# The end of a two-layer streaming encoder: second half of the tokens turned by TensorE before the last scaling

## The chip, the cores and the metric

One core of a Trainium2 chip runs the whole kernel. Its engines are TensorE (PE, matmuls), VectorE (DVE), ScalarE (ACT), GpSimd (POOL) and SyncE (SP, which here only issues DMAs). Each takes its instructions in the order in which they were written. The metric is the device time of one launch in microseconds (us), the median of several runs.

## The reference

The input is x, 512 tokens by 1024 features, in float32. Two layers follow, each a token mixer and a gated feed-forward network (FFN), both behind an RMS norm and both added to x. The last norm gives the output:

```python
def rmsnorm(x, g):
    xf = x.astype(jnp.float32)
    y = xf * lax.rsqrt(jnp.mean(xf * xf, axis=-1, keepdims=True) + EPS)
    return (y * g.astype(jnp.float32)).astype(x.dtype)

def conv_ffn(h, w_up, conv_w, conv_b, w_down):
    u, v = jnp.split(h @ w_up, 2, axis=-1)
    u = causal_dwconv(u, conv_w, conv_b)
    return (jax.nn.gelu(u, approximate=False) * v) @ w_down

for l in range(2):
    x = x + mixer(rmsnorm(x, mix_norm[l]))
    x = x + conv_ffn(rmsnorm(x, ffn_norm[l]), ...)
return rmsnorm(x, final_norm)
```

So every token needs the sum of the squares of its 1024 features, its inverse root, and then each feature is multiplied by that root and by the feature's gain in final_norm.

## The kernel before

The kernel keeps x with the features on the partitions: eight tiles x[0] to x[7] of 128 features by 512 tokens, all in one buffer xall (x3 is its view as 8 tiles). Every product is done in three matmul passes on high and low parts of the operands (accumulate, L252, and seven_product). Weights are loaded, split into the two parts and used block by block.

The work of the FFN is an order written out by hand: each step is entered with a time by at(t, step), and run_plan sorts the steps by these times and issues them. The order of the instructions of TensorE, VectorE and ScalarE is thereby fixed. Loads and stores that SP issues are queued in the order in which they are written.

At the end of the second FFN the down-projection makes the eight feature tiles one after the other. Each is multiplied by the norm factors rs and added to x[j] (add_x, L810 and L811). Then finish(j) is called, which for this layer is last(j, half). For the tiles 0 to 6 that squares x[j] and adds the squares to acc (square_acc, L288 and L289). For the tiles 0 to 5, x[j] is also multiplied by its gain, in place, on ScalarE (L1480).

The last tile, x[7], is made in two halves of 256 tokens (down_half): 42 matmuls for the first half, then add_x and last(7, 0) for it, then 42 matmuls for the second half, add_x and last(7, 1). In last(7, half):

- ScalarE squares the half tile (L1483). PE sums the columns of acc and of these squares over the partitions by a matmul with ones (L1490), giving two columns of 128 sums, tokens on partitions.
- rsqrt_small takes the inverse root: VectorE makes v (L293), ScalarE a first y (L295), and three small VectorE instructions refine it (L299 to L301).
- spread_small (L327) multiplies by an identity on PE so that the root of each token stands on all partitions (bc).
- scale_out multiplies pairs of feature tiles by it on VectorE (L1514; for the tiles 6 and 7, whose gain is still missing, L1517) and stores each pair, 256 KB, in rows of 256 tokens (L1520).

Work can be put between the matmuls: after(n, fn) runs fn at the n-th tick from now, and down_half ticks once for each group of seven matmuls. For the first half the sums and the root are put behind 2 groups and the spread behind 4, so they stand between the matmuls of the second half. The scaling of the first half is issued in last(7, 1): two pairs ahead of the second half's root, one between its steps and one behind it.

Of the kernel before, what the change touches and what calls it, by code (L numbers as in the profile page):

```python
# [7 lines left out]
F32 = mybir.dt.float32  # L8
# [3 lines left out]
AF = mybir.ActivationFunctionType  # L12
ALU = mybir.AluOpType

P = 128
T = 512
D = 1024
KD = D // P
# [7 lines left out]
EPS = 1e-6  # L26
# [29 lines left out]
NPLAIN = NF - KD  # L56
# [15 lines left out]


@with_exitstack
def trunk_kernel(ctx, tc, xT, cols, gain0, w_lead, w_ab, w_pool, w_abo, w_vg, w_qk, w_r, w_g2, w_go, w_up, w_dn, w_ds, outT):
    nc = tc.nc
    V, S, G, PE = nc.vector, nc.scalar, nc.gpsimd, nc.tensor

# [5 lines left out]
    sp = ctx.enter_context(tc.tile_pool(name="sp", bufs=2))  # L84
    ps = ctx.enter_context(tc.tile_pool(name="ps", bufs=8, space=bass.MemoryType.PSUM))

    def slot(dt=F32, name="s"):
        return big.tile([P, T], dt, tag="s", name=name)
# [17 lines left out]
    def bank(name="ps"):  # L106
        return ps.tile([P, T], F32, tag="ps", name=name)
# [3 lines left out]
    x = [xall[:, k * T : (k + 1) * T] for k in range(KD)]  # L111
# [4 lines left out]
    def col(name, i=0):  # L116
        c = COLS[name] + i
        return colt[:, c : c + 1]
# [30 lines left out]
    ones = cp.tile([P, P], F32, tag="ones", name="ones")  # L149
# [5 lines left out]
    warm = ps.tile([P, T], F32, tag="ps", name="warm")  # L155
# [6 lines left out]
    eps_t = cp.tile([P, 1], F32, tag="eps", name="eps_t")  # L162
# [3 lines left out]
    ident = cp.tile([P, P], F32, tag="ident", name="ident")  # L166
# [77 lines left out]
    def after(n, fn):  # L244
        pending.append((done[0] + n, fn))
# [6 lines left out]
        for p in due:  # L252
            p[1]()

    def accumulate(out, wh, wl, ah, al, first=True, last=True, step=None, cut=0, loose=False):
        n = len(ah)
        if cut:
            accumulate(out, wh, wl, ah[:cut], al[:cut], first, False)
            accumulate(out, wh[:, cut:, :], wl[:, cut:, :], ah[cut:], al[cut:], False, last)
            return  # L260
        for i, (w, a) in enumerate(((wh, ah), (wh, al), (wl, ah))):
            for k in range(n):
                PE.matmul(  # L263
                    out, w[:, k, :], a[k], start=first and i == 0 and k == 0, stop=last and i == 2 and k == n - 1,
                    skip_group_check=loose,
                )
            if step:
                step()

# [13 lines left out]
    def square_acc(k, acc, ts=slice(0, T)):  # L283
        if k == 0 and ts.start == 0:
            S.activation(acc[:, ts], x[0][:, ts], AF.Square)
            return
        sq = slot(name="sq")
        S.activation(sq[:, ts], x[k][:, ts], AF.Square)  # L288
        V.tensor_tensor(acc[:, ts], acc[:, ts], sq[:, ts], ALU.add)  # L289

    def rsqrt_small(dst, ssum, n, width, between=None):
        v = sp.tile([P, n], F32, tag=f"v{n}", name="v")
        V.tensor_scalar(v, ssum, 1.0 / width, EPS, ALU.mult, ALU.add)  # L293
        y = sp.tile([P, n], F32, tag=f"y{n}", name="y")
        S.activation(y, ssum, AF.Abs_reciprocal_sqrt, bias=eps_t, scale=1.0 / width)  # L295
        if between:
            between()
        t = sp.tile([P, n], F32, tag=f"t{n}", name="t")
        V.tensor_tensor(t, y, v, ALU.mult)  # L299
        V.scalar_tensor_tensor(t, t, -0.5, y, ALU.mult, ALU.mult)  # L300
        V.scalar_tensor_tensor(dst, t, 1.5, y, ALU.add, ALU.mult)  # L301
# [22 lines left out]
    def spread_small(y, n):  # L324
        b = bank("bc")[:, : n * P]
        for c in range(n):
            PE.matmul(  # L327
                b[:, c * P : (c + 1) * P], y[:, c : c + 1].broadcast_to([P, P]), ident, start=True, stop=True
            )
        return b  # L330
# [28 lines left out]
    def conv3(u, wname, bname, j, nj):  # L359
        tap = conv_steps(u, wname, bname, j, nj)  # L360
        return [tap(i) for i in range(3)][0]

    def scaled(o, rs, tag):
        u = slot(name=tag)
        V.tensor_tensor(u, o, rs, ALU.mult)
        return u
# [244 lines left out]
    def ffn(l, acc, mixed, finish, ahead, halves_last=False):  # L611
# [141 lines left out]
        o, late, ops = {}, {}, {}  # L753
# [8 lines left out]
        def down_half(half, k0, kt):  # L762
            if half == 0:
                late[k0] = ready.pop(0)
            h, lo = late[k0]
            ts = slice(half * H, half * H + H)
            if k0 == 0:
                o["half"] = bank("dn")
            accumulate(
                o["half"][:, :H], h, lo,  # L770
                [m[:, ts] for m in mh[k0 : k0 + kt]], [m[:, ts] for m in ml[k0 : k0 + kt]],
                k0 == 0, k0 + kt == NPLAIN, step=tick,
            )

        def down_seven(p, base):
# [53 lines left out]
        t = base + 9 * UNIT  # L829
# [3 lines left out]
        def plain_down(j):  # L833
            nonlocal t
            while blocks and (blocks[0][0] == j or (j == 0 and blocks[0][0] < 4)):
                jj, k0, kt = blocks.pop(0)
                first = t < base + 9.5 * UNIT
                block(t - 16.0, t - (9.3 if first else 6.0), t - (7.0 if first else 4.5))
                if halves_last and jj == KD - 1:
                    at(t, lambda a=(0, k0, kt): down_half(*a))  # L840
                    t += 1.5 * kt * MM
                else:
                    at(t, lambda a=(jj, k0, kt): down(*a))
                    t += 3 * kt * MM
# [26 lines left out]
        if halves_last:  # L871
            at(t, lambda: add_x(KD - 1, o["half"][:, :H], lo_t))
            at(t, lambda: finish(KD - 1, 0))
            for k0, kt in zip(DOWN_AT, DOWN_K):
                at(t, lambda a=(1, k0, kt): down_half(*a))
                t += 1.5 * kt * MM
            at(t, lambda: add_x(KD - 1, o["half"][:, :H], hi_t))
            at(t, lambda: finish(KD - 1, 1))
        else:
            done_right(HK - 1, t + 0.3)  # L880
# [5 lines left out]
    acc = slot(name="acc")  # L886
# [30 lines left out]
    with tc.manual_schedule(engines=set(planned)):  # L917
# [6 lines left out]
        for n in range(2, 5):  # L924
            k = lead[n][1]
# [62 lines left out]
    for j in range(4):  # L988
        pc = project(xh, xl, "pc") if j else first_pc
        px = project(xh, xl, "px")  # L990
        c = scaled(pc, rs, "u")
        d = scaled(px, rs, "v")
        V.tensor_tensor(c, c, d, ALU.mult)
        a = conv3(c, "sc_w", "sc_b", j, 4)
        pb = project(xh, xl, "pb")
        b = scaled(pb, rs, "v")
        V.tensor_tensor(b, b, a, ALU.mult)
        split(y_h[4 + j], y_l[4 + j], b)
    acc = slot(name="acc")
# [13 lines left out]
    acc = total[0]  # L1013
# [273 lines left out]
    t = 0.0  # L1287
# [15 lines left out]
    first = True  # L1303
    for b, (n, ks) in enumerate(zip(VG_COLS, VG_K)):
        k0 = 0
# [158 lines left out]
    acc = slot(name="acc")  # L1464
# [3 lines left out]
    mixed = mix_out("go", "ffn1", acc, 2, 2)  # L1468

    squares = []  # L1470

    def last(j, half=None):
        if not squares:
            squares.append(slot(name="acc"))
        acc = squares[0]
        ts = slice(0, T) if half is None else slice(half * 256, half * 256 + 256)
        if half is None:
            square_acc(j, acc)
            if j < KD - 2:
                S.activation(x[j], x[j], AF.Copy, scale=col("fin", j))  # L1480
            return
        sq = slot(name="sq")[:, :256]
        S.activation(sq, x[j][:, ts], AF.Square)  # L1483
        y2 = sp.tile([P, 2], F32, tag="y2", name="y2")

        def one(between=None):
            b = bank("ss")
            for i, t in enumerate((acc[:, ts], sq)):
                for c in range(2):
                    PE.matmul(  # L1490
                        b[:, c : c + 1], t[:, c * P : (c + 1) * P], ones[:, 0:1],
                        start=i == 0 and c == 0, stop=i == 1, skip_group_check=True,
                    )
            rsqrt_small(y2, b[:, :2], 2, D, between)

        def two():
            return ts, spread_small(y2, 2)

        if half:
            scale_out(*spread[0], (0, 2))  # L1500
            one(lambda: scale_out(*spread[0], (4,)))
            scale_out(*spread[0], (6,))
            scale_out(*two(), range(0, KD, 2))
        else:
            after(2, one)
            after(4, lambda: spread.append(two()))

    spread = []

    def scale_out(ts, b, ks):  # L1510
        for k in ks:
            o3 = x3[:, k : k + 2, ts]
            if k < KD - 2:
                V.tensor_tensor(o3, o3, b[:, None, :].broadcast_to([P, 2, 256]), ALU.mult)  # L1514
            else:
                for i in range(2):
                    V.scalar_tensor_tensor(  # L1517
                        x[k + i][:, ts], x[k + i][:, ts], col("fin", k + i), b, ALU.mult, ALU.mult
                    )
            (nc.scalar if k % 4 and ts.start else nc.sync).dma_start(  # L1520
                outT[k * P : (k + 2) * P, ts].rearrange("(a p) t -> p a t", p=P), o3
            )

    ffn(1, acc, mixed, last, 0, True)


_OUTS = [((D, T), "float32")]


def _blocks(w, n):  # L1530
# [72 lines left out]
```

## Time and profile before

| | |
|---|---|
| median of 3 runs | 1003.15 us (1002.39 to 1003.23) |
| profiled execution | 1002.91 us |
| its span | 1001.0 us |
| mean granted TensorE clock | 0.996 of full speed |
| busy, share of the span | PE 99%, DVE 85%, ACT 61%, POOL 9% |

A profile records one execution. Its span runs from the first to the last recorded instruction; 1.9 us of the execution's time lie outside it. In timelines a row gives the start and the duration in us, the engine, the line and operation, the tiles (out<-in) with their shapes and the number of instructions that were merged; in brackets stands how long the engine was idle before and what released it. SPq and ACTq are the queues from which SP and ScalarE issue DMAs. A matmul's recorded duration contains its way through the array, so rows of consecutive matmuls overlap.

### The profile page before, as it was taken

How to read it: one execution, taken by the hardware profiler on the slowest of the kernel's cores; microseconds unless marked ns; L12 is line 12 of the kernel's file. 1: busy time of each engine (PE TensorE's matmuls, PEld its weight loads, DVE VectorE, ACT ScalarE, POOL GpSimd, SP SyncE). 2: the span in 40 equal slices, each digit the busy share in tenths (PEclk: the TensorE clock that was granted, in tenths of full speed). 3: DMA queues.
4: the chain of work that ended last, by engine and by line, in shares of the span. 5: the costliest groups of instructions: out<-in, count | busy, mean ns of one | idle time of the engine just before them, and what ended most of it. 6: DMA issues, size and time to landing. Idle time of an engine off the chain costs nothing.

```text
span 1001.0 us, 18094 instructions
## 1 busy us (share of the span) xinstructions
PE 990.2 (99%) x7180; PEld 930.1 (93%) x7180; DVE 855.8 (85%) x1285; ACT 608.1 (61%) x991; POOL 86.4 (9%) x109
## 2 busy tenths in 40 slices
PE   9999999999999999999999999999999999999996
PEld 7888889999999988899999999899999999988896
DVE  7886689999999997767879789889999999997775
ACT  6432567767676764445876576667676676755451
POOL 0000111111111000002000000110110111000000
PEclk9999999999999999999999999999999999999998
DMA  7433757788777454527335553868788778354522
GB/s 247 139 92 105 187 119 181 200 202 203 190 206 183 134 127 137 136 85 194 92 105 133 122 124 110 207 144 196 190 212 197 190 199 195 121 137 135 129 80 84
DMA packets 66116, 154.39 MB, mean 154 GB/s; under 512 B 5648, under 2 KB 8080, under 8 KB 66032
## 3 DMA queue, kind: packets, MB, share of 16 engines
q1 hardware_dynamic: 47584, 118.63, 37.8%
q0 software_dynamic: 17760, 34.08, 20.8%
q8 instruction: 56, 0.92, 0.4%
q10 hardware_dynamic: 688, 0.53, 0.2%
q14 instruction: 28, 0.23, 0.1%
HBM read 148.50 MB, written 2.10 MB: 150 GB/s over the span
## 4 chain that ended last, share of the span: by engine, by line
PE 98%; DVE 2%; issue 0%; ACT 0%; DVEq 0%; ACTq 0%
PE stx L533 32%; PE styz L533 19%; PE dn L263 15%; PE go L263 4%; PE abo L263 4%; PE pu L912 2%; PE pc L263 2%; PE dn L533 2%; PE pb L263 2%; PE px L263 2%; PE stz L533 2%; PE vg L1119 2%; PE vg L1121 1%; PE vg L1120 1%; PE o L1210 1%; PE stw L533 1%
## 5 line engine op out<-in xcount | busy, mean ns | idle before, releaser
L485 DVE TENSOR_TENSOR lo<-raw,hi 128x1024 fp32r<-128x1024 f32 x120 | 146.4, 1220 | 19.1 <-ACT hi L479 18.8
L479 ACT ACTIVATE hi<-raw 128x1024 fp32r<-128x1024 f32 x120 | 125.5, 1058 | 28.4 <-PE styz L533 11.3
L461 POOL DMA_DIRECT2D s<-in_w_up x44 | 53.1, 1207 | 474.5 <-DVE u L652 102.2
L222 DVE TENSOR_TENSOR lo<-raw,hi 128x1024 fp32r<-128x1024 f32 (+3 forms) x69 | 78.9, 1145 | 9.5 <-ACT hi L218 9.0
L218 ACT ACTIVATE hi<-raw 128x1024 fp32r<-128x1024 f32 (+3 forms) x69 | 68.3, 991 | 26.4 <-PE px L263 9.0
L354 DVE SCALAR_TENSOR_TENSOR cacc<-u,colt,cacc 128x511 f32<-128x511 f32 x96 | 71.5, 744 | 2.6 <-ACT cacc L351 2.5
L485 DVE TENSOR_TENSOR lo<-s,hi 128x1024 fp32r<-128x1024 f32 x60 | 73.1, 1218 | 0.0
L351 ACT ACTIVATE cacc<-u,colt 128x512 f32<-128x512 f32 x48 | 39.2, 817 | 44.9 <-DVE u L655 41.3
L533 PE MATMUL stx<-th,hi 128*128 128x256 f32 x416 | 64.5, 277 | 0.0
L533 PE MATMUL stx<-tl,hi 128*128 128x256 f32 x416 | 64.1, 276 | 0.0
L533 PE MATMUL stx<-th,lo 128*128 128x256 f32 x416 | 64.1, 276 | 0.0
L479 ACT ACTIVATE hi<-s 128x1024 fp32r<-128x1024 f32 x60 | 63.3, 1055 | 0.8
L533 PE MATMUL styz<-xh,lo 128*128 128x256 f32 x400 | 61.8, 276 | 0.7 <-DVE lo L485 0.7
L533 PE MATMUL styz<-xh,hi 128*128 128x256 f32 x400 | 62.0, 277 | 0.0
L533 PE MATMUL styz<-xl,hi 128*128 128x256 f32 x400 | 61.6, 276 | 0.0
L479 ACT ACTIVATE sh<-raw 128x512 fp32r<-128x512 f32 x60 | 38.0, 633 | 30.8 <-DVE raw L490 30.8
L263 PE MATMUL dn<-mh,hi 128*128 128x512 f32 (+1 forms) x238 | 56.5, 377 | 0.0
L263 PE MATMUL dn<-mh,lo 128*128 128x512 f32 (+1 forms) x238 | 56.4, 376 | 0.0
L263 PE MATMUL dn<-ml,hi 128*128 128x512 f32 (+1 forms) x238 | 56.4, 376 | 0.0
L533 PEld LDWEIGHTS stx<-th,hi 128*128 128x128 f32 x416 | 54.9, 188 | 0.6 <-ACT k L640 0.3
L533 PEld LDWEIGHTS stx<-tl,hi 128*128 128x128 f32 x416 | 54.9, 188 | 0.0
L533 PEld LDWEIGHTS stx<-th,lo 128*128 128x128 f32 x416 | 54.9, 188 | 0.0
(342 smaller groups left out, 2553.6 us busy)
## 6 DMA issues: line engine op xcount, KB each, us to landing
s<-in_w_up SPq DMA_DIRECT2D x44, 512.0 KB, 6.9
s<-in_w_up POOLq DMA_DIRECT2D x44, 512.0 KB, 7.2
raw<-in_w_up SPq DMA_DIRECT2D x44, 512.0 KB, 6.6
raw<-in_w_dn SPq DMA_DIRECT2D x32, 448.0 KB, 3.4
raw<-in_w_up SPq DMA_DIRECT2D x44, 256.0 KB, 3.5
raw<-in_w_ab SPq DMA_DIRECT2D x12, 512.0 KB, 3.6
raw<-in_w_abo SPq DMA_DIRECT2D x8, 512.0 KB, 3.6
s<-in_w_ds SPq DMA_DIRECT2D x8, 512.0 KB, 6.4
```

The lines of the kernel that those rows point to most:

```text
L218: S.activation(parts[0], raw, AF.Copy)
L222: V.tensor_tensor(parts[1], raw, f32(parts[0]), ALU.subtract)
L263: PE.matmul(out, w[:, k, :], a[k], start=first and i == 0 and k == 0, stop=last and i == 2 and k == n - 1, skip_group_check=loose,)
L351: S.activation(acc[0], u, AF.Identity, bias=col(bname, j), scale=col(wname, 2 * nj + j))
L354: V.scalar_tensor_tensor(a, u[:, : T - i], col(wname, (2 - i) * nj + j), a, ALU.mult, ALU.add)
L461: G.dma_start(w["s31"].rearrange("p (a n) -> p a n", a=2), part, accum_op=ALU.add)
L479: S.activation(h, src(), AF.Copy)
L485: V.tensor_tensor(lo, src(), f32(h), ALU.subtract)
L533: PE.matmul(b[out][:, ts], wt[:, ks[k]], a[k], start=first and i == 0 and k == 0, stop=i == 2 and k == HK - 1, skip_group_check=True,)
L912: PE.matmul(pus[g], parts[k][w][:, g * P : (g + 1) * P], a[k], start=k == 0 and i == 0, stop=k == KD - 1 and i == 2,)
L1119: PE.matmul(o[c][:, :n], xh[kk][:, cs], h[:, k, :], start=kk == 0, stop=False)
L1120: PE.matmul(o[c][:, :n], xl[kk][:, cs], h[:, k, :], start=False, stop=False)
```

## The change

The output becomes two arrays in one: the first 256 tokens as before, features by tokens, and the other 256 as tokens by features. The host puts them together.

First half: last(6) also multiplies x[6] by its gain, and a dummy instruction loads ScalarE's table for the inverse root there. last(7, 0) multiplies the half of x[7] by its gain. down_half now ticks at each matmul; sums and root stand behind 14 matmuls, as before, the spread behind 25 instead of 28. With the spread, three pairs of tiles are scaled and stored. The fourth pair follows in last(7, 1).

Second half: the gain of x[7] goes to a tile xf. PE transposes all eight feature tiles, 128 tokens at a time, into four PSUM banks: ten transposes ahead of the column sums, six behind. The root stays on the tokens' partitions as y2. ScalarE and VectorE multiply a bank each by a column of y2, twice, and the four results of 128 tokens by 512 features are stored, three from SP and one from ScalarE. The new function root computes the inverse root without v.

```diff
-    def accumulate(out, wh, wl, ah, al, first=True, last=True, step=None, cut=0, loose=False):
+    def accumulate(out, wh, wl, ah, al, first=True, last=True, step=None, cut=0, loose=False, each=None):
...
+                if each:
+                    each()
...
-                k0 == 0, k0 + kt == NPLAIN, step=tick,
+                k0 == 0, k0 + kt == NPLAIN, each=tick,
...
+    first_out = out[0]
+    second_out = out[1].rearrange("(t a) b -> t (a b)", a=KD // 2)
+    tokens = []
...
         if half is None:
             square_acc(j, acc)
-            if j < KD - 2:
-                S.activation(x[j], x[j], AF.Copy, scale=col("fin", j))
+            S.activation(x[j], x[j], AF.Copy, scale=col("fin", j))
+            if j == KD - 2:
+                table = sp.tile([P, 1], F32, tag="warm", name="warm", bufs=1)
+                S.activation(table, ones[:, 0:1], AF.Abs_reciprocal_sqrt)
             return
...
-        def two():
-            return ts, spread_small(y2, 2)
-
-        if half:
-            scale_out(*spread[0], (0, 2))
-            one(lambda: scale_out(*spread[0], (4,)))
-            scale_out(*spread[0], (6,))
-            scale_out(*two(), range(0, KD, 2))
-        else:
-            after(2, one)
-            after(4, lambda: spread.append(two()))
...
+        def root():
+            y = sp.tile([P, 2], F32, tag="v2", name="y")
+            t = sp.tile([P, 2], F32, tag="t2", name="t")
+            S.activation(y, b[0][:, :2], AF.Abs_reciprocal_sqrt, bias=eps_t, scale=1.0 / D)
+            V.scalar_tensor_tensor(t, b[0][:, :2], D * EPS, y, ALU.add, ALU.mult)
+            V.scalar_tensor_tensor(t, t, -0.5 / D, y, ALU.mult, ALU.mult)
+            V.scalar_tensor_tensor(y2, t, 1.5, y, ALU.add, ALU.mult)
+
+        if half == 0:
+            S.activation(x[j][:, ts], x[j][:, ts], AF.Copy, scale=col("fin", j))
+
+            def both():
+                part(0, acc[:, ts])
+                part(1, sq)
+                root()
+
+            def spread():
+                tokens.append(spread_small(y2, 2))
+                scale_first((0, 2, 4))
+
+            after(14, both)
+            after(25, spread)
+            return
+        xf = slot(name="xf")[:, :256]
+        V.tensor_scalar(xf, x[j][:, ts], col("fin", j), None, ALU.mult)
+        scale_first((6,))
+        to = [[bank("to") for e in range(2)] for c in range(2)]
+
+        def turn(k):
+            for c in range(2):
+                at = ts.start + c * P
+                src = xf[:, c * P : (c + 1) * P] if k == j else x[k][:, at : at + P]
+                PE.transpose(to[c][k // 4][:, k % 4 * P : k % 4 * P + P], src, ident)
+
+        for k in range(5):
+            turn(k)
+        part(0, acc[:, ts])
+        part(1, sq)
+        for k in range(5, KD):
+            turn(k)
+        root()
+        for c in range(2):
+            res = [slot(name="res") for e in range(2)]
+            S.activation(res[0], to[c][0], AF.Copy, scale=y2[:, c : c + 1])
+            V.tensor_scalar(res[1], to[c][1], y2[:, c : c + 1], None, ALU.mult)
+            for e in range(2):
+                queue = nc.scalar if c and e else nc.sync
+                queue.dma_start(second_out[c * P : (c + 1) * P, e * T : (e + 1) * T], res[e])
+
+    def scale_first(ks):
+        ts, b = slice(0, 256), tokens[0]
         for k in ks:
             o3 = x3[:, k : k + 2, ts]
+            V.tensor_tensor(o3, o3, b[:, None, :256].broadcast_to([P, 2, 256]), ALU.mult)
+            nc.sync.dma_start(first_out[k * P : (k + 2) * P, :].rearrange("(a p) t -> p a t", p=P), o3)
...
-_OUTS = [((D, T), "float32")]
+_OUTS = [((2, D, T // 2), "float32")]
...
-    return np.ascontiguousarray(o.T)[None]
+    return np.concatenate([o[0].T, o[1].reshape(T // 2, D)])[None]
```

More of the change, by code (lines that the diff above doesn't have):

```diff
@@ L74, in trunk_kernel @@
 @with_exitstack
-def trunk_kernel(ctx, tc, xT, cols, gain0, w_lead, w_ab, w_pool, w_abo, w_vg, w_qk, w_r, w_g2, w_go, w_up, w_dn, w_ds, outT):
+def trunk_kernel(ctx, tc, xT, cols, gain0, w_lead, w_ab, w_pool, w_abo, w_vg, w_qk, w_r, w_g2, w_go, w_up, w_dn, w_ds, out):
     nc = tc.nc
@@ L1475, in last @@
         acc = squares[0]
-        ts = slice(0, T) if half is None else slice(half * 256, half * 256 + 256)
         if half is None:
             square_acc(j, acc)
-            if j < KD - 2:
-                S.activation(x[j], x[j], AF.Copy, scale=col("fin", j))
+            S.activation(x[j], x[j], AF.Copy, scale=col("fin", j))
+            if j == KD - 2:
+                table = sp.tile([P, 1], F32, tag="warm", name="warm", bufs=1)
+                S.activation(table, ones[:, 0:1], AF.Abs_reciprocal_sqrt)
             return
+        ts = slice(half * 256, half * 256 + 256)
         sq = slot(name="sq")[:, :256]
@@ L1484, in last @@
         y2 = sp.tile([P, 2], F32, tag="y2", name="y2")
[L1486 to L1494, printed above, removed]
-        def two():
-            return ts, spread_small(y2, 2)
@@ L1499, in last, with part @@
-        if half:
-            scale_out(*spread[0], (0, 2))
-            one(lambda: scale_out(*spread[0], (4,)))
-            scale_out(*spread[0], (6,))
-            scale_out(*two(), range(0, KD, 2))
-        else:
-            after(2, one)
-            after(4, lambda: spread.append(two()))
-    spread = []
-    def scale_out(ts, b, ks):
+        b = []
+        def part(i, t):
+            if not b:
+                b.append(bank("ss"))
+            for c in range(2):
+                PE.matmul(
+                    b[0][:, c : c + 1], t[:, c * P : (c + 1) * P], ones[:, 0:1],
+                    start=i == 0 and c == 0, stop=i == 1, skip_group_check=True,
+                )
@@ new lines, in last @@
+        part(0, acc[:, ts])
[3 more added lines that the diff above has]
+        root()
+        for c in range(2):
+            res = [slot(name="res") for e in range(2)]
[4 more added lines that the diff above has]
+                queue.dma_start(second_out[c * P : (c + 1) * P, e * T : (e + 1) * T], res[e])
@@ L1511, in scale_out @@
+    def scale_first(ks):
+        ts, b = slice(0, 256), tokens[0]
         for k in ks:
             o3 = x3[:, k : k + 2, ts]
[L1513 to L1522, printed above, removed]
+            V.tensor_tensor(o3, o3, b[:, None, :256].broadcast_to([P, 2, 256]), ALU.mult)
+            nc.sync.dma_start(first_out[k * P : (k + 2) * P, :].rearrange("(a p) t -> p a t", p=P), o3)
```

## The prediction, made before the changed kernel was run

> **What bounds the kernel now.** I read the page first, then the chain of waits of the last 26 us, then the timeline of that stretch on all engines, then the DMA rates in short windows. The page says which engine the span is made of.
>
> ```profile
> span 1001.0 us, 18094 instructions
> ...
> PE 98%; DVE 2%; issue 0%; ACT 0%; DVEq 0%; ACTq 0%
> ```
>
> TensorE carries 98% of the chain that ended last, and the diff leaves all of its work up to the last down-projection alone. So the change can only move what lies behind the last matmul, a tail of some 11 us. The chain shows its links (start, us, what):
>
> ```profile
> 988.39 1.65 PE dn L263 x14
> 990.04 0.02 issue
> 990.07 0.45 DVE dn L810
> 990.51 0.02 issue
> 990.53 0.42 DVE xall L811
> 990.96 1.19 DVE xall L1514 x2
> ...
> 992.26 0.59 DVE xall L1514
> ...
> 993.16 0.17 DVE y L301
> 993.33 0.04 issue
> 993.38 1.24 PE bc L327 x4
> 994.62 0.02 issue
> 994.64 0.69 DVE xall L1514
> ```
>
> The last matmul ends at 990.04. VectorE adds x (to 990.95), then scales the first half of the tokens in between; the root of the second half is ready at 993.33, PE spreads it over all partitions (1.24 us), and only at 994.64 does the first scaling of the second half begin. What follows is output traffic. The two issues are the first and the last of the second half (timeline); the windows give, in their last two columns, the DMA engines' busy share and GB/s, and ahead of them TensorE's granted clock.
>
> ```profile
> 995.35 0.37 SPq L1520 DMA_DIRECT2D out<-xall  x1
> ...
> 997.34 0.38 ACTq L1520 DMA_DIRECT2D out<-xall  x1
> ```
>
> ```profile
> 8.00:10.00 2.00, 2.00 (x10) 1.67 (x9) 0.70 (x1) 0.87 (x1) 0.00 (x0) 1.00 1.03 402
> 10.00:12.00 2.00, 2.00 (x10) 1.65 (x10) 1.78 (x2) 2.00 (x5) 0.00 (x0) 1.00 1.02 399
> 992.20:992.50 0.30, 0.00 (x0) 0.00 (x0) 0.30 (x2) 0.14 (x1) 0.00 (x0) 1.00 0.01 3
> 992.80:993.10 0.30, 0.00 (x0) 0.00 (x0) 0.27 (x3) 0.00 (x0) 0.00 (x0) 0.50 1.03 321
> 996.20:999.40 3.20, 0.00 (x0) 0.00 (x0) 1.10 (x3) 0.00 (x0) 0.00 (x0) 0.50 0.97 328
> 999.20:999.40 0.20, 0.00 (x0) 0.00 (x0) 0.00 (x0) 0.00 (x0) 0.00 (x0) 0.50 0.67 226
> ```
>
> The row 996.20 to 999.40 is the reading that matters: 3.20 us at 328 GB/s are 1.05 MB, all of the second half, back to back, with the DMA engines 97% busy. The last 0.2 us are two thirds full, so the bytes run from about 996.25 (0.90 after the issue at 995.35) to 999.33, 3.08 us at 340 GB/s; 1.67 us of landing and closing steps end the span. The four issues are some 0.65 us apart and each moves 0.77 us of data: the stage is bound by when its first store is issued and by how fast the four run, not by when the last scaling is done.
>
> **The change, part by part.** Three things happen: the root of the first half moves off a table load, the first half's scaling moves ahead of the last addition, and the second half's path loses the spread on PE and gains transposes.
>
> First half. Its rows now:
>
> ```profile
> 984.81 0.42 ACT L1483 ACTIVATE sq<-xall 128x256 f32<-128x256 f32 x1 [3.84 <-DVE xall L811]
> 985.24 1.28 ACT L295 ACT_TABLE_LOAD   x1
> ...
> 985.63 0.58 PE L1490 MATMUL ss<-ones,sq 128*128 128x1 f32 x4
> ...
> 986.54 0.26 ACT L295 ACTIVATE y<-ss,eps_t 128x2 f32<-128x2 f32 x1
> ...
> 987.23 0.16 DVE L301 SCALAR_TENSOR_TENSOR y<-t,y 128x2 f32<-128x2 f32 x1
> ...
> 987.79 0.60 PE L327 MATMUL bc<-ident,y 128*128 128x128 f32 x4
> ...
> 989.06 0.97 PE L263 MATMUL dn<-mh,lo 128*128 128x256 f32 x7
> ```
>
> The table load, with a gain copy of x[6] (0.72 us, row of L1480 below), moves into the 3.84 us that ScalarE idles before 984.81: 2.3 us of work, at no cost; without that gap it would cost up to 1.28. The root then waits only for the sums (985.63 + 0.58 = 986.21): 986.25 + 0.26, and 0.59 from there to the end of L301 as now (986.80 to 987.39), is 987.10. The spread is put 25 matmuls behind the call instead of 28, three times 0.113 us earlier (seven matmuls take 0.79): it would start at 987.45 and end at 988.05. The root is there 0.2 us before PE asks. If it were not, PE would stall and 17 down matmuls with it; I price that at 0 to 0.2. Then VectorE scales three pairs; the row below has three in 1.88 us, so it is free at 989.95, 0.1 us before L810 starts at 990.07. VectorE's queue is in order, so a spread late by more than 0.1 delays the last addition by the rest: 0 taken, 0 to 0.3 as bounds. Their three stores go to SP's queue from about 988.7 and have it to themselves; the fourth pair's store, issued about 992.2, has its bytes moved by 993.9.
>
> ```profile
> 990.99 0.42 ACT L1483 ACTIVATE sq<-xall 128x256 f32<-128x256 f32 x1 [4.19 <-DVE xall L811]
> 991.46 0.61 PE L1490 MATMUL ss<-ones,sq 128*128 128x1 f32 x4 [1.09 <-ACT sq L1483]
> ...
> 992.11 0.16 DVE L293 TENSOR_SCALAR v<-ss 128x2 f32<-128x2 f32 x1
> ...
> 992.36 0.26 ACT L295 ACTIVATE y<-ss,eps_t 128x2 f32<-128x2 f32 x1 [0.95 <-DVE v L293]
> ...
> 994.64 1.88 DVE L1514 TENSOR_TENSOR xall<-xall,bc 128x512 f32<-128x512 f32 x3 [0.53 <-PE bc L327]
> ```
>
> Second half. The addition still ends at 990.95 and the squares at 991.41. PE now has ten transposes in its queue ahead of the two column sums. The trace has transposes of this shape:
>
> ```profile
> 616.40 1.04 PE L1256 MATMUL yt<-ident,ot 128*128 128x128 f32 x8
> 617.20 0.60 PE L533 MATMUL styz<-xh,hi 128*128 128x256 f32 x3
> ```
>
> Eight take 0.80 us until the next matmul starts, 0.10 each. From 989.85 (989.06 and seven times 0.113) ten end at 990.85, the sum over acc (about 0.5) at 991.4, just when the squares arrive: 0 taken, 0.1 as bound. The sums end at 992.07 as now. Six transposes more end at 992.7 at full clock; the granted clock falls to 0.50 between 992.5 and 992.8 in the rows above, and even at half speed throughout they end at 993.3, 0.3 behind the root, hurting only the second tiles. The gain of x[7] (L1517's form, 0.475) and the last first-half scaling (0.68) keep VectorE until 992.13. The root no longer computes v: y, which now waits for DVE v, starts at 992.11 instead of 992.36, ends at 992.37, and 0.59 later, 992.96, the root is there (993.33 now). The spread (1.24) is gone. Instead ScalarE and VectorE read the turned tokens from PSUM:
>
> ```profile
> L1315 ACT ACTIVATE rs<-bc 128x512 f32<-128x512 f32 x1 | 0.6, 600 | 0.5 <-PE bc L327 0.5
> L1480 ACT ACTIVATE xall<-xall,colt 128x512 f32<-128x512 f32 x6 | 4.3, 724 | 0.2
> L1067 DVE TENSOR_SCALAR z<-z,colt 128x512 f32<-128x512 f32 x4 | 2.8, 745 | 0.2 <-PE z L1065 0.2
> L1517 DVE SCALAR_TENSOR_TENSOR xall<-xall,colt,bc 128x256 f32<-128x256 f32 x4 | 1.7, 475 | 0.0
> ```
>
> ScalarE: between 0.600 (from PSUM, no column) and 0.724 (with a column as scale); I take 0.70. VectorE: 0.745, a column operation out of PSUM. The first tile is done at 993.00 + 0.70, so its store is issued at 993.72 where it is 995.35 now: 1.63 us earlier (bounds 1.75 with the short ScalarE row; 1.2 with all the waits above). Second pair of tiles: done at 994.4 and 994.5. SP issues at 0.38 us each, so the last store starts by 994.55 and its bytes could flow from 995.45, long before its turn: the four run back to back again.
>
> How fast: now the stores go in pieces of 256 floats, 1 KB, at 340 GB/s. The second half becomes pieces of 512 floats, 2 KB. No store of that size is in the trace. Below stands the 340; above, the loads at the start, which mix 2-KB pieces (x) and 4-KB pieces (weights) and run at 402, with the 4-KB weights alone at 399. I take 400, nearest by size, though a load: 1.049 MB take 2.62 instead of 3.08, 0.46 less (bounds 0 and 0.5). The Trainium skill (DMA: Bandwidth & Descriptors, "Why small descriptors are slow") counts three cycles of overhead for every packet of 32-byte beats, 35 cycles for 1 KB and 67 for 2 KB; by that the data would take 2.95 us. The trace disagrees on the size: 399 at 4 KB against 340 at 1 KB is 17%, where that count makes 7%.
>
> Sum: 1.63 + 0.46 = 2.09. The profiled execution took 1002.91 (span 1001.0, 1.9 around it), which gives 998.9 and 1000.8. The profiled execution lies 0.24 under the median of 1003.15, so the forecast for the median is 1001.1.
>
> **The rivals.** 0.2% is 2.0 us, about what a measurement of this kernel tells from no change; the forecast lies on that line.
>
> Stores no faster in 2-KB pieces: the path is 1.63 shorter and nothing else, 1001.5, within 0.2%. For it: the only stores in the trace run at 340 with the engines 97% busy, and a load says little of a write. Against: the engines are as busy at 402. The page's count above gives 1.76 and the same verdict.
>
> VectorE late: if the root or the spread of the first half comes 0.5 us later than I work out, the three scalings, now ahead of L810 in its in-order queue, push the last addition and all behind it: gain 1.6, and more lateness takes as much more; 1001.5 to 1002.2. For it: only 0.1 us of slack. Against: each duration in that count has its own row.
>
> Slower: the turning costs what PE's other f32 work on 128 columns costs. Row L327 has two such matmuls in 0.60 us at full clock, 1.24 at half, 0.3 and 0.6 each. Then ten last 3.0, the sums end 1.6 us late (993.7) and the clock has fallen, so six more last 3.7: 997.4. The second tiles are scaled at 998.1, half a megabyte follows (0.9 and 1.3) and the closing 1.7: 1002.0, 1.0 slower, 1004.2 for the median. It decides for slower from about 0.5 us per transpose. Against: L1256 shows 0.10 for this form on PE.
>
> The change not doing what it says: the transposes could wait on the scalings of other tokens in the same xall buffer. Its row shows the contrary:
>
> ```profile
> 994.13 0.37 SPq L1520 DMA_DIRECT2D out<-xall  x1
> ```
>
> L1514 writes second-half tokens from 994.64 on, while this store of first-half tokens, whose bytes start 0.90 after its issue, has still to read the same buffer: parts are tracked apart; and even a wait for the last first-half scaling (992.13) would be hidden. No price.
>
> **How the numbers follow.** Forecast 0.55 (with 2.0 reached in 0.47 and just missed in 0.08), the path and rate both better than taken 0.05, stores at 340 0.22, VectorE late 0.08, slower 0.10. So faster 0.52, same 0.38, slower 0.10. The range: the best bounds give 1.75 + 0.5 = 2.25 or 1000.9; the three runs lie up to 0.8 from their median, of which I allow 0.5 below, 1000.4. The lateness case reaches 1002.2, and 0.3 above it is 1002.5. The forecast's own range is 1000.7 to 1001.5.
>
> **What would show it.** Right: no ACT_TABLE_LOAD after 984; three L1514-type scalings ended before the dn addition, which still starts near 990.1; ten transposes in about 1 us; the first second-half store near 993.7; its data in one stretch of 2.6 us; span near 998.9. Wrong: the dn addition later than 990.3; transposes of 0.3 us; a table load behind 990; or the four stores at 340 GB/s or slower.

## The result

Over 22 runs each the median went from 1003.24 to 1001.70 us: ratio 0.9985, 95% interval 0.9979 to 0.9991, about 1.5 us or 0.15%. (One of the 22 runs of before took 4831 us; it does not move the median.) That is within 0.2%; the forecast was 1001.1 (range 1000.4 to 1002.5). Twelve runs of the same kernel in another job gave 1001.46 and a ratio of 0.9978 (0.9964 to 0.9993).

The profiled execution after took 1001.93 us, with this on its page:

```profile
span 999.9 us, 18119 instructions
```

The span fell by 1.1 us only. The chain of waits of after runs over the same PE work as before up to the last matmul, which ends 0.89 us later, and then over other links (start, us, what):

```profile
988.94 1.98 PE dn L263 x17
990.93 1.09 PE to L1535 x10
992.02 0.96 PE ss L1498 x8
992.98 0.02 issue
993.00 0.27 ACT y L1506
...
993.69 0.17 DVE y L1509
...
993.96 0.75 DVE res L1547
```

The spread on PE (1.24 us) is gone from it, and from the root at 993.85 it goes straight to the tiles that are stored. The timeline of after shows the first half's work between the matmuls and the stores:

```profile
982.61 1.28 ACT L1486 ACT_TABLE_LOAD   x1
...
988.34 0.60 PE L329 MATMUL bc<-ident,y 128*128 128x128 f32 x4
...
988.98 1.88 DVE L1556 TENSOR_TENSOR xall<-xall,bc 128x512 f32<-128x512 f32 x3 [0.99 <-PE bc L329]
...
990.96 0.43 DVE L812 TENSOR_TENSOR dn<-dn,rs 128x256 f32<-128x256 f32 x1
...
993.88 1.27 ACT L1546 ACTIVATE res<-to,y 128x512 f32<-128x512 f32 x2 [0.62 <-DVE y L1509]
...
994.60 1.33 SPq L1550 DMA_DIRECT2D out<-res  x3
```

The windows show the second half's data (last columns: DMA share, GB/s):

```profile
990.80:992.60 1.80, 1.80 (x18) 1.72 (x17) 1.63 (x5) 0.42 (x1) 0.00 (x0) 1.00 1.03 343
995.60:998.20 2.60, 0.00 (x0) 0.00 (x0) 0.00 (x0) 0.00 (x0) 0.00 (x0) 0.75 1.01 379
998.20:998.40 0.20, 0.00 (x0) 0.00 (x0) 0.00 (x0) 0.00 (x0) 0.00 (x0) 0.50 0.20 62
```

The first row is the first half, in pieces of 1 KB: 343 GB/s. The second is the second half, in pieces of 2 KB: 379. Its 1.05 MB take 2.77 us, from 995.46 to 998.23.

To compare ends without what happened ahead of them I use the tail: from the start of the product with rs for the first half of x[7], which is the first of the two rows dn<-dn,rs (983.88 before, 984.77 after), to the end of the span. It fell from 17.12 to 15.13 us, by 1.99. The other 0.89 lie ahead. There PE, VectorE and GpSimd have the same instructions in the same order in both kernels, and ScalarE has them up to 981.9, where the gain of x[6] and the table load come in. Two weight loads landed later in the profile of after; the first row is before, the others are after and its chain there:

```profile
722.88 1.06 ACT L479 ACTIVATE hi<-raw 128x1024 fp32r<-128x1024 f32 x1 [0.25 <-DMA raw<-in_w_up]
```

```profile
724.70 1.07 ACT L481 ACTIVATE hi<-raw 128x1024 fp32r<-128x1024 f32 x1 [1.68 <-DMA raw<-in_w_up]
```

```profile
716.57 8.05 DMA raw<-in_w_up
...
724.70 1.07 ACT hi L481
...
727.93 3.00 PE stx L535 x24
```

ScalarE waits 1.68 us for the block where it waited 0.25, and PE loses about 0.5 us there.

### The profile page after: what moved, and what is told of

Its sections match the earlier page's. It is cut to its first block, busy times and chain, and to the rows that moved or that the text cites. A ratio compares the mean times of both kernels' runs of the same rounds, so it can differ in the third digit from the quotient of the medians.

```text
span 999.9 us, 18119 instructions
## 1 busy us (share of the span) xinstructions
PE 991.5 (99%) x7192; PEld 931.5 (93%) x7192; DVE 855.4 (86%) x1280; ACT 610.4 (61%) x996; POOL 86.3 (9%) x109
## 4 chain that ended last, share of the span: by engine, by line
PE 93%; DVE 4%; ACT 1%; issue 1%; DMA 1%; DVEq 0%; ACTq 0%
PE stx L535 30%; PE styz L535 17%; PE dn L263 15%; PE go L263 4%; PE abo L263 4%; PE pu L914 2%; PE pc L263 2%; PE dn L535 2%; PE pb L263 2%; PE px L263 2%; PE stz L535 2%; PE vg L1121 2%; PE vg L1123 1%; PE vg L1122 1%; DVE lo L487 1%
## 5 line engine op out<-in xcount | busy, mean ns | idle before, releaser
L535 PE MATMUL stx<-th,hi 128*128 128x256 f32 x416 | 64.8, 278 | 0.2 <-ACT kk L642 0.2
L535 PE MATMUL stx<-tl,hi 128*128 128x256 f32 x416 | 64.1, 276 | 0.0
L535 PE MATMUL stx<-th,lo 128*128 128x256 f32 x416 | 64.1, 276 | 0.0
L535 PE MATMUL styz<-xh,lo 128*128 128x256 f32 x400 | 61.8, 276 | 0.7 <-DVE lo L487 0.7
L535 PE MATMUL styz<-xh,hi 128*128 128x256 f32 x400 | 62.0, 277 | 0.0
L535 PE MATMUL styz<-xl,hi 128*128 128x256 f32 x400 | 61.6, 276 | 0.0
L535 PEld LDWEIGHTS stx<-th,hi 128*128 128x128 f32 x416 | 54.9, 188 | 1.1 <-ACT kk L642 0.6
L535 PEld LDWEIGHTS stx<-tl,hi 128*128 128x128 f32 x416 | 54.9, 188 | 0.0
L535 PEld LDWEIGHTS stx<-th,lo 128*128 128x128 f32 x416 | 54.9, 188 | 0.0
```

Of the source, the lines that this page charges most:

```text
L535: PE.matmul(b[out][:, ts], wt[:, ks[k]], a[k], start=first and i == 0 and k == 0, stop=i == 2 and k == HK - 1, skip_group_check=True,)
```

## The experiments

The tail is given beside the time, since it depends less on what happened ahead of it. Spans are read to 0.1 us, so a tail is good to about 0.05.

**The changed kernel again** (nothing edited).

> The changed kernel, nothing edited. The tail, from the start of the product with rs for the first half of x[7] to the end of the span, was 17.1 us before and 15.1 after in the two profiles; the work ahead of that point ended 0.89 us later in the profile of after, where two weight loads landed late. Theory A (that difference is chance of one execution): tail 15.1 again, the point ahead of it anywhere from 983.5 to 985, and over many runs about 2.0 us faster than before (ratio near 0.998). Theory B (the change slows the work ahead of the tail): tail 15.1, the point again near 984.8, and about 1.2 us faster (ratio near 0.9988).

Tail 15.11; it starts at 984.49. The ratio of 0.9978 is on the side of theory A, with an interval that holds both.

**The kernel before again, twice** (nothing edited).

> The kernel before, nothing edited. Tail (from the start of the product with rs for the first half of x[7] to the end of the span) 17.1 us. Five profiles of kernels with parts of the change reached that point at 984.5 to 985.7, the one profile of before at 983.88. Theory A (chance of one execution): this profile reaches it anywhere from 983.5 to 985.7. Theory B (the change slows the work ahead of the tail, though the order of instructions there is the same): 983.9 again.

> The kernel before once more, for a third profile. Its tail was 17.1 with TensorE's clock at 0.50 under the spread of the second half (1.23 us) and 16.75 with the clock at 1.00 (0.71 us): one of the two again, by the clock. The start of the tail was at 983.9 both times and at 984.3 to 985.7 in eight kernels with the change: if that is chance, 984.0 or later is as likely as not.

The tail starts at 983.95 and, the third time, at 984.87. So the kernel before also has late starts. The third time it even has the same late block as the profile of after, with a wait of 1.59 us:

```profile
724.70 1.06 ACT L479 ACTIVATE hi<-raw 128x1024 fp32r<-128x1024 f32 x1 [1.59 <-DMA raw<-in_w_up]
```

What lies ahead of the tail is thus chance of one execution as far as three profiles can show. With all profiles of the change at 984.3 or later (985.1 on the mean, against 984.2 for the three of before) a small shift stays possible.

The eleven runs of the first of these two gave 1002.87 us and a ratio of 0.9984 (0.9968 to 1.0000) to the other runs of the same kernel in that job. Nothing differs between the two, so a ratio from some ten runs is not safe to 0.2%, and what is said below of the single parts rests on the tails.

The tail was not 17.1 each time but 16.75 and 17.23, which the expectation for the first of the two had missed. The rows of the spread, first in the second profile of before, then in the third, show why, with the granted clock in the windows after them (second profile; first profile):

```profile
993.44 0.71 PE L327 MATMUL bc<-ident,y 128*128 128x128 f32 x4 [1.31 <-DVE y L301]
```

```profile
994.37 1.22 PE L327 MATMUL bc<-ident,y 128*128 128x128 f32 x4 [1.31 <-DVE y L301]
```

```profile
992.50:994.40 1.90, 0.71 (x4) 0.52 (x4) 1.81 (x7) 0.19 (x1) 0.00 (x0) 1.00 0.97 327
```

```profile
993.40:994.60 1.20, 1.20 (x4) 0.90 (x4) 0.70 (x2) 0.00 (x0) 0.00 (x0) 0.50 1.01 346
```

PE is nearly idle from the last matmul on. In one execution the clock is still full when the spread comes (0.71 us), in two it has halved (1.2). The changed kernel has no such spread, so its tail is the same either way.

**Each part alone.** First the moved scaling without the turning:

```diff
-        xf = slot(name="xf")[:, :256]
-        V.tensor_scalar(xf, x[j][:, ts], col("fin", j), None, ALU.mult)
+        S.activation(x[j][:, ts], x[j][:, ts], AF.Copy, scale=col("fin", j))
         scale_first((6,))
...
+        b2 = spread_small(y2, 2)
+        for k in range(0, KD, 2):
+            o3 = x3[:, k : k + 2, ts]
+            V.tensor_tensor(o3, o3, b2[:, None, :256].broadcast_to([P, 2, 256]), ALU.mult)
+            queue = nc.scalar if k % 4 else nc.sync
+            queue.dma_start(out[1][k * P : (k + 2) * P, :].rearrange("(a p) t -> p a t", p=P), o3)
```

> The first part of the change alone: first half scaled ahead of the last addition, root without v, table early; second half spread by PE and scaled and stored by feature tiles as before. If the turning carries most of the gain: first second-half store 0.7 to 1.4 us later than in the changed kernel, data at 340 GB/s, tail 16.1 to 16.7. Rival (the moved scaling carries it): tail 15.5 or less.

Tail 16.25, ratio 1.0003 (0.9981 to 1.0025). The first second-half store is issued 10.6 us after the start of the tail, against 9.8 in the changed kernel. This kernel still spreads the second half's root on PE, and in this profile the clock was full there:

```profile
994.77 0.71 PE L329 MATMUL bc<-ident,y 128*128 128x128 f32 x4 [0.94 <-DVE y L1509]
```

```profile
994.70:995.60 0.90, 0.71 (x4) 0.52 (x4) 0.10 (x2) 0.00 (x0) 0.00 (x0) 1.00 0.43 141
```

So the profile of before to hold against it is the second one, with a tail of 16.75 and a spread of 0.71 us too: the moved scaling alone saves 0.5 us.

Then the turning without the moved scaling:

```diff
                 tokens.append(spread_small(y2, 2))
-                scale_first((0, 2, 4))
...
-        scale_first((6,))
+        scale_first((0, 2, 4, 6))
```

> The second part alone: second half turned, but the first half's four pairs are scaled behind the last addition, ahead of the second half's root. If VectorE's order matters: four scalings of 0.63 us hold the root back by 1.4 us, first second-half store 1.4 us later, tail 16.5. Rival (the scalings hide behind the sums and the stores): tail 15.3 or less.

Tail 16.53, ratio 0.9985 (0.9965 to 1.0005). Timeline:

```profile
992.46 2.47 DVE L1555 TENSOR_TENSOR xall<-xall,bc 128x512 f32<-128x512 f32 x4
...
993.12 0.64 PE L1534 MATMUL to<-ident,xall 128*128 128x128 f32 x4
...
993.30 0.26 ACT L1506 ACTIVATE y<-ss,eps_t 128x2 f32<-128x2 f32 x1 [0.70 <-PE ss L1498]
...
995.23 0.16 DVE L1509 SCALAR_TENSOR_TENSOR y<-t,y 128x2 f32<-128x2 f32 x1
...
996.14 0.83 SPq L1549 DMA_DIRECT2D out<-res  x2
```

Four scalings keep VectorE until 994.9, y has been there since 993.6, and the root follows only then. Against the 16.75 of before with the clock full, the moved scaling alone gives 0.5 us, the turning alone 0.2, and both together 1.6: neither part, as it was run, carries the gain. With VectorE held like this the turning loses 1.4 us of tail against the changed kernel.

That the turning needs the moved scaling is not shown by this. In the kernel before only two of the four pairs stand ahead of the second half's root; here all four do. With two ahead, VectorE would have been free at about 993.7 (an estimate from 992.46 and two times 0.62), 0.1 us behind y. The turning with that order was not run, and might keep most of the gain.

**The size of the stored pieces.**

```diff
-    second_out = out[1].rearrange("(t a) b -> t (a b)", a=KD // 2)
+    second_out = out[1].rearrange("(s t) b -> t s b", s=4)
...
-                queue.dma_start(second_out[c * P : (c + 1) * P, e * T : (e + 1) * T], res[e])
+                queue.dma_start(second_out[c * P : (c + 1) * P, 2 * e : 2 * e + 2, :], res[e].rearrange("p (s b) -> p s b", s=2))
```

> Changed kernel with the second half's four stores in pieces of 1 KB instead of 2 KB (another order of the output in memory, the same bytes). If the size of the pieces sets the rate: second-half data 3.1 us at about 340 GB/s instead of 2.8, tail 15.4. If it does not, 2.8 us and 15.1.

Tail 15.54, and its windows:

```profile
995.60:998.40 2.80, 0.00 (x0) 0.00 (x0) 0.00 (x0) 0.00 (x0) 0.00 (x0) 0.61 1.03 340
998.40:998.60 0.20, 0.00 (x0) 0.00 (x0) 0.00 (x0) 0.00 (x0) 0.00 (x0) 0.50 0.49 159
```

340 GB/s again: for the same bytes the size of the pieces sets the rate, and the 2-KB pieces are worth 0.4 us of the tail. The time does not show it: median 1002.12, ratio 0.9978 (0.9959 to 0.9997), the same ratio as the changed kernel's in that job.

**The slacks.** Three kernels take one cover away each: the early table load,

```diff
-            if j == KD - 2:
-                table = sp.tile([P, 1], F32, tag="warm", name="warm", bufs=1)
-                S.activation(table, ones[:, 0:1], AF.Abs_reciprocal_sqrt)
```

> Changed kernel without the dummy instruction that loads ScalarE's table early. If the load was hidden only because it was moved: it lands ahead of y of the first half, the root comes 0.8 us later, PE waits about 0.6 us for it with 17 down matmuls behind, tail 15.7. Rival (slack covers it): 15.1 to 15.2.

the three matmuls by which the spread comes earlier,

```diff
-            after(25, spread)
+            after(28, spread)
```

> Changed kernel with the spread behind 28 matmuls, as before, instead of 25. The three scalings ahead of the last addition end 0.34 us later, about 991.2 on the changed kernel's clock, where the addition starts at 990.96: if VectorE's slack is 0.1 as worked out, tail 15.35. Rival (the addition is bound elsewhere): 15.1.

and the place of four transposes.

```diff
-        for k in range(5):
+        for k in range(7):
...
-        for k in range(5, KD):
+        for k in range(7, KD):
```

> Changed kernel with fourteen transposes ahead of the column sums instead of ten. If PE's order was just filled (ten end when the squares arrive), four more hold the sums by up to 0.4 us; but the last pair ahead, of x[6], is not held by VectorE's scaling of the first half of x[6], since other tokens. Tail 15.5. Rival (slack on PE): 15.1.

Tails 15.75, 15.34 and 15.42, all as expected to 0.1. The times (medians 1002.43 and 1002.28, and a single run at 1001.89) do not tell them from the changed kernel. With the spread behind 28 the last addition starts 6.36 us after the start of the tail instead of 6.19:

```profile
985.56 0.43 DVE L812 TENSOR_TENSOR dn<-dn,rs 128x256 f32<-128x256 f32 x1 [1.66 <-PE dn L263]
...
991.92 0.43 DVE L812 TENSOR_TENSOR dn<-dn,rs 128x256 f32<-128x256 f32 x1
```

Of the 0.34 us, 0.17 reached the addition, so VectorE's slack was 0.17 and not 0.1.

Without the early load the timeline has the table ahead of y and PE waiting for the root, with the dn matmuls queued behind:

```profile
987.36 1.28 ACT L1503 ACT_TABLE_LOAD   x1
...
989.55 0.71 PE L329 MATMUL bc<-ident,y 128*128 128x128 f32 x4 [0.37 <-DVE y L1506]
```

**Two scalings per stored tile.** Each bank now holds feature tiles such that both engines work on the same stored tile:

```diff
-                PE.transpose(to[c][k // 4][:, k % 4 * P : k % 4 * P + P], src, ident)
+                at = k // 4 * 256 + k % 2 * P
+                PE.transpose(to[c][k // 2 % 2][:, at : at + P], src, ident)
...
-            S.activation(res[0], to[c][0], AF.Copy, scale=y2[:, c : c + 1])
-            V.tensor_scalar(res[1], to[c][1], y2[:, c : c + 1], None, ALU.mult)
+                S.activation(res[:, :256], to[c][0][:, part_e], AF.Copy, scale=y2[:, c : c + 1])
+                V.tensor_scalar(res[:, 256:], to[c][1][:, part_e], y2[:, c : c + 1], None, ALU.mult)
```

> A version meant to be better: each stored tile of 128 tokens by 512 features is scaled by both engines at once, ScalarE the first 256 features from one PSUM bank, VectorE the other 256 from another, so that the first store is issued after 0.40 us of scaling instead of 0.70. The four stores are bound by their own data from the first issue on, so the end moves with it: tail 14.8. Rival (issue spacing or the later scalings bind): 15.1.

A miss: tail 15.09. Timeline of that kernel:

```profile
993.23 0.16 DVE L1509 SCALAR_TENSOR_TENSOR y<-t,y 128x2 f32<-128x2 f32 x1
993.48 0.48 ACT L1549 ACTIVATE res<-to,y 128x256 f32<-128x256 f32 x1 [0.67 <-DVE y L1509]
993.50 0.48 DVE L1550 TENSOR_SCALAR res<-to,y 128x256 f32<-128x256 f32 x1
```

A half as wide costs 0.48 and not 0.40, and starts 0.09 after the root where the whole one started 0.03 after it. The first store is issued 9.74 us into the tail instead of 9.83. The other 0.05 is no more than the rounding of the spans. The ratio, 0.9968 (0.9949 to 0.9988), does not separate it from the changed kernel.

**The root for 128 tokens at a time.** The core of the edit, first with new small tiles:

```diff
+        for c in range(2) if half else ():
+            S.activation(sq[:, c * P : (c + 1) * P], x[j][:, ts.start + c * P : ts.start + c * P + P], AF.Square)
...
+        ys = [sp.tile([P, 1], F32, tag=f"y1{c}", name="y") for c in range(2)]
+        for c in range(2):
+            S.activation(ys[c], s2[c][:, :1], AF.Abs_reciprocal_sqrt, bias=eps_t, scale=1.0 / D)
+        for c in range(2):
+            t1 = sp.tile([P, 1], F32, tag="t1", name="t")
+            y = ys[c]
+            V.scalar_tensor_tensor(t1, s2[c][:, :1], D * EPS, y, ALU.add, ALU.mult)
+            V.scalar_tensor_tensor(t1, t1, -0.5 / D, y, ALU.mult, ALU.mult)
+            V.scalar_tensor_tensor(y2[:, c : c + 1], t1, 1.5, y, ALU.add, ALU.mult)
```

> A version meant to be better: in the second half squares, column sums and root are made for 128 tokens at a time, so that the first 128 tokens need half the squares and half the sums before their root. The last square is 0.14 us shorter and two column sums (0.22 us) fall out ahead of the first root; the second root follows while the first tiles are scaled and stored. First second-half store 0.36 us earlier, tail 14.75 instead of 15.1. Rival (VectorE, with six small steps instead of three, or PE holds it): 15.0 or more.

Tail 14.9, yet 1027.84 us, ratio 1.0231 (1.0205 to 1.0257). The groups by line, this kernel first and then the changed one, have the reason:

```profile
L535 PE MATMUL stx<-th,hi 128*128 128x256 f32 x416 | 66.6, 282 | 0.0
```

```profile
L535 PE MATMUL stx<-th,hi 128*128 128x256 f32 x416 | 64.8, 278 | 0.2 <-ACT kk L642 0.2
```

Matmuls far ahead of the edit take longer, in the same order. Summed over the trace, from each one's start to the next, the 5040 matmuls of L535 take 600.8 us instead of 576.4. What the edit can change there is where the tiles lie: three new small tiles in an early pool would move those behind. The same steps in slices of the tiles that exist:

```diff
-        ys = [sp.tile([P, 1], F32, tag=f"y1{c}", name="y") for c in range(2)]
+        y = sp.tile([P, 2], F32, tag="v2", name="y")
+        t = sp.tile([P, 2], F32, tag="t2", name="t")
```

> The root for 128 tokens at a time again, but in small tiles that the kernel has already, so that no tile ahead of the tail moves in SBUF. In the version with three new small tiles the tail was 14.8 us, and the matmuls of the feed-forward layers took 283 instead of 276 ns, some 26 us in all, with the same order of instructions there. If the place of the tiles is what cost this: matmuls of 276 ns, start of the tail between 983.9 and 985.7, tail 14.8, about 2.2 us faster than before. Rival (something else in that version): slow by some 25 us again.

Median 1001.21, ratio 0.9974 (0.9951 to 0.9997), tail 14.84, and matmuls as in the changed kernel:

```profile
L535 PE MATMUL stx<-th,hi 128*128 128x256 f32 x416 | 64.6, 278 | 0.0
```

The sum over L535 is 575.8 us. So the three new tiles cost the 25 us. That they do it by moving other tiles is the explanation left, since ahead of the tail the instructions are the same; where the tiles lie was not looked at. This version has the shortest tail of all, 0.3 us under the changed kernel's; its time is not told apart from it.

## Why the prediction came out as it did

The direction, the path and the range held; the most likely case, faster by just over 0.2%, did not, since 1.5 us were measured for 2.09. The sum itself is tested by the tail, which fell by 1.99 in the first pair of profiles.

The path, step by step, with the prediction's times moved by the 0.89 us of the late start:

| | predicted | measured |
|---|---|---|
| three scalings end | 990.84 | 990.86 |
| addition starts | 990.96 | 990.96 |
| column sums end | 992.96 | 992.97 |
| root ready | 993.85 | 993.85 |
| first second-half store issued | 994.61 | 994.60 |
| its data end | 998.13 | 998.23 |

So the term of 1.63 us for the first store was right, and so were the covers: the table load in ScalarE's gap, ten transposes beside the addition, the slack on VectorE. The three slack experiments show that each of these covers was needed; VectorE's, at 0.17 us, was a little wider than the 0.1 worked out.

The term that was mis-sized is the rate of the stores. 400 GB/s was taken from loads; the 2-KB stores ran at 379, so 0.31 us were saved instead of 0.46. One reading behind the 400 was wrong too: the row from 10 to 12 us, taken for 4-KB weights alone, has over half of its bytes in 2-KB pieces. So its 399 is no rate of 4-KB pieces, and the 17% between 4 and 1 KB falls with it. Between 11 and 12 nearly all pieces are 2 KB:

```profile
11.00:12.00 1.00, 1.00 (x6) 0.84 (x5) 1.00 (x2) 1.00 (x3) 0.00 (x0) 1.00 1.03 395
```

So with pieces of 2 KB loads ran at 395 and stores at 379. The 400 was good for a load and too high for a store; why stores are slower is not shown. The rival in which they stay at 340 was wrong: the 1-KB experiment puts them back to 340 and costs 0.4. The Trainium skill (DMA: Bandwidth & Descriptors, "Why small descriptors are slow") gives each packet a fixed overhead of about three cycles, so that larger pieces run faster; the trace agrees on the direction. By an estimate from that figure the data would have taken 2.95 us; the trace says 2.77.

The second thing was not in the sum at all: what the change is measured against. The prediction took the spread's 1.24 us at half clock, in the one profile it had, as a constant of the kernel. In another execution of the same kernel it took 0.71 and the tail 16.75. The saving of 1.99 is thus measured against a profile in which this step took long. Against the three tails of before (17.12, 16.75, 17.23) the 15.1 of after are 1.6 to 2.1 less. The Trainium skill (TensorE: Matmul & The Clock Gate, "Part 1: The HAM clock gate") says that the window after which an idle PE is throttled runs free; the clock that had fallen ahead of the spread in two profiles (1.24 and 1.22 us) and not in the third (0.71) agrees with that. No run here shows the window itself.

What remains between those 1.6 to 2.1 us and the 1.5 of the first 22 runs is within the interval (0.9 to 2.1 us), and the second job's 0.9978 lies on the other side. The start of the tail scatters by 2.4 us (983.9 to 986.3) over the profiles of all kernels but the one with slower matmuls, though PE's work ahead of it is the same in all, so no more can be said from these runs. How close the measured median came to the forecast is therefore in part luck.

Of the other rivals, VectorE was late only where it was made late; a transpose took 0.11 us (ten in 1.09), not 0.3; and parts of xall were tracked apart: in the run with the turning alone, four transposes ran from 993.12 on, beside the scalings of 992.46 to 994.93.

## What to carry to other kernels

Where the end is a row of stores, count from the issue of the first and multiply by a rate for their piece size: starting them earlier and making the pieces larger both counted in full here (1.64 and 0.31 of the 1.99 us). Whether finishing only the last computation earlier gains anything was not tried. When a step is moved into a gap or ahead of another in an in-order queue, work out the slack from rows; here 0.34 us more delay cost 0.15 to 0.2, and the table load outside its gap 0.62. Compare ends from a common point inside the kernel when the expected gain is as small as the scatter of what runs ahead, and take more than one profile of the kernel before: here one step of its tail took 0.71 us in one profile and 1.2 in two.

## What the runs showed of the hardware that was not expected

Three small tiles, declared at the end of the program, made every run 26 us slower (1027.84 against 1001.21 with the same steps in existing tiles): the group of feed-forward matmuls shown went from a mean of 278 to 282 ns in an unchanged order, and all matmuls of that line together took 25 us more. Why was not tried.

Stores of 2-KB pieces ran at 379 GB/s and of 1-KB pieces at 340 to 343, with the DMA engines as busy in both (shares of 1.01 and 1.03).
